# 48 in place of 32 blocks of the expert table u beside the selection, and 1.2 row fetches with each in place of 1.1

## The chip, the cores and the metric

The kernel runs on one core of one Trainium2 chip. Its time is in device microseconds from the start of the program to its end; three runs gave 3198.60, 3206.87 and 3208.08 us, so the median is 3206.87 us. The engines are named as the profile names them: PE is TensorE (PEld its weight loads), DVE is VectorE, ACT is ScalarE, POOL is GpSimd, and SP only issues transfers.

## The reference

One layer of a sequence model on 512 rows of width 2048, all in float32. A projection feeds a short convolution and a matrix memory, a second projection and a layer norm follow. The last part, in which the change lies, is a product-key lookup ("PEER"): for each row and each of 8 heads, 16 experts out of 16384 are picked by two top-16 searches over 128 keys; then

```
q  = h @ wq;  s = q . keys;  top 16 x top 16 -> top 16 experts eid, gate = softmax(top_s)
act = gelu(u[eid] . h)              # u: 16384 x 2048
ff  = sum over heads, experts of (gate * act) * v[eid]     # v: 16384 x 2048
out = LN(2^(1/4) * h + ff)
```

## The kernel before

The lookup is done in two ways at once. For 288 of the 512 rows ("columns" of the products) the kernel doesn't gather: it multiplies all of u with them, block by block (128 blocks of 128 experts), takes the gelu, multiplies it by a dense weight matrix that holds the gate of the picked experts and zero elsewhere, and multiplies the result with all of v. For the other 224 rows (128 of the first row tile, 64 and 32 of the second) it fetches the 128 picked rows of u and of v from HBM by indirect DMA, one fetch of 128 rows (1 MB) per slot, and DVE forms the dot product (line 558) or adds the weighted row (line 571). These fetches are a list of jobs, 462 with some others, and `advance(n)` issues n more of them after each block of the products, wherever the kernel is by then.

Every product is done in three passes, high times high, low times high, high times low. So each 1 MB block of a weight goes through `load_split`: a transfer on SP's queue (line 101), ACT rounds it to `hi` (line 109), DVE subtracts to get `lo` (line 110), and PE does 16 x 3 matmuls of 288 columns on it (lines 116 to 118).

The program has these stretches at the place of the change:

- The top-16 searches, on DVE, up to about 1230 us.
- The **selection stage** (1227 to about 1645 us). It multiplies the first `AHEAD` blocks of u (`u_chunk`), writes their gelu to DRAM (`hs_d`, line 904), and beside each block it takes some jobs from a second list: three `select` (DVE), three `spread`, and 72 *builds*. A build makes the weight matrix for 4 columns: DVE compares (line 848, `oa`) and scales (line 851, `ob`) one-hot matrices in bf16, PE multiplies them in 12 matmuls (line 858), ACT copies the result (line 861). After every 8 builds a 2 MB store goes to DRAM (line 896). The second list is taken by a power of the block's number: `len(jobs) * ((c + 1) / (AHEAD - 1)) ** 1.4`, so it is empty one block before the last.
- `MORE` = 4 more blocks of u, and then the **product stage** (to about 3120 us): 15 groups of 8 blocks of v (`v_part`), 4 more pieces of v, and the rest of u between them. Each of these is a *turn* that ends with `advance(rest / (turns - 4))`, `rest` being the slot jobs that are left.

`group_chunks` pairs the blocks that were done ahead with later ones: a group of v needs 8 blocks of gelu, and in the first `(AHEAD + MORE) / 4` groups 4 of them come back from DRAM (line 942) and 4 are multiplied in the group before; in later groups all 8 are. So a group of the first sort has 12 turns (8 of v, 4 of u), one of the second sort 16.

The order of instructions on an engine is not the order of the code: a scheduler lays out each engine's queue from priorities (the split of a block has a raised priority, `PRIO`) and estimated times, and the engines then run in that order. Fetches are tied to the last product in front of them for that layout alone.

The loop of the selection stage:

```
for c in range(AHEAD):
    gl = u_chunk(c, t2)
    nc.scalar.dma_start(hs_d[c], gl)
    upto = min(len(jobs), int(len(jobs) * min(1.0, (c + 1) / (AHEAD - 1)) ** POW + 1e-6))
    while done < upto:
        jobs[done]()
        done += 1
    advance(RATE_MID, 2 * NSLOT)
```

Of the kernel before, what the change touches and what calls it, by code (L numbers as in the profile page):

```python
# [37 lines left out]
TGRP = [(0, REST), (REST, P), (REST + P, P)]  # L38
TG = 32
NTG = ND // TG  # L40
AHEAD = 32
MORE = 4
NSLOT = 128
GL = 4
# [2 lines left out]
PRIO = 1000  # L47
LAG = 6
RATE_PROJ = 1.9
RATE_MID = 1.1  # L50
VW = P + 1
HK = NH * TOPK

# [1 line left out]
def group_chunks():  # L55
    cut = AHEAD + MORE
    gs = [list(range(4 * g, 4 * g + 4)) + list(range(cut + 4 * g, cut + 4 * g + 4)) for g in range(cut // 4)]
    gs += [list(range(c, c + 8)) for c in range(2 * cut, 120, 8)]
    return gs + [list(range(120, 124))]
# [6 lines left out]
def tile_kernel(ctx: ExitStack, tc: tile.TileContext, x, lin_g, lin_b, w_rows, w_proj, w_v, w_gate, b_gate,  # L66
# [17 lines left out]
    w_d = dram.tile([NTG, P, NKEY * TG], F32, name="w_d")  # L84
    hs_d = dram.tile([AHEAD + MORE, P, ND], F32, name="hs_d")
    nM_d = dram.tile([NH, S], F32, name="nM_d")
# [493 lines left out]
    def advance(n, most=10 ** 9):  # L580
        done_jobs[1] = min(done_jobs[1] + n, most, len(sjobs))
        while done_jobs[0] < int(done_jobs[1]):
            sjobs[done_jobs[0]]()
            done_jobs[0] += 1
# [190 lines left out]
    def u_chunk(c, pool, nb=2):  # L775
        w = load_split(ut[c])
        ps = ph.tile([P, S], F32, name="ph")
        for k in range(KD):
            mm3(ps[:, :ND], [a[:, k * P:(k + 1) * P] for a in w], [a[:, k, DS] for a in h1T], k == 0, k == KD - 1)
        gl = pool.tile([P, ND], F32, name="gl", bufs=nb)  # L780
        ACT.activation(gl, ps[:, :ND], AF.Gelu)  # L781
        return gl

    with ExitStack() as p2:
# [116 lines left out]
        done = 0  # L901
# [9 lines that stand above are left out]
    with ExitStack() as p3:  # L911
# [19 lines left out]
        def load_w(g):  # L931
            t_ = g2.tile([P, NTG, 4, TG], F32, name="wt")
            nc.sync.dma_start(t_.rearrange("p g i t -> p g (i t)"),
                              w_d[:, :, g * 4 * TG:(g + 1) * 4 * TG].rearrange("g p f -> p g f"))
            wt[g] = t_

        def make_g(c):
            if c // 4 not in wt:
                load_w(c // 4)
            if c < AHEAD + MORE:  # L940
                gl = g2.tile([P, ND], F32, name="gl", bufs=GL)
# [88 lines left out]

        for c in range(AHEAD, AHEAD + MORE):
            nc.scalar.dma_start(hs_d[c], u_chunk(c, g2, GL))
# [142 lines left out]
```

## Time and profile before

| what | value |
|---|---|
| median of three runs | 3206.87 us |
| profiled execution, its own time | 3204.96 us |
| its span, first to last instruction | 3203.2 us |
| PE busy | 2941.0 us, 92% |
| DVE busy | 2784.5 us, 87% |
| ACT busy | 1153.6 us, 36% |
| moved by DMA | 1013.19 MB, mean 316 GB/s |

Busy time of an engine is the time in which at least one of its instructions is in flight. A matmul of 288 columns is shown with some 300 ns, but the next begins long before it ends, so a row's mean duration is not what one costs; the distance between the ends of two blocks is. A window of the trace gives for each engine the busy time and the count of instructions, then the clock that PE was granted (1.00 is 2.4 GHz, 0.50 is 1.2 GHz), the busy share of the 16 DMA engines and what they moved.

### The profile page before, as it was taken

To read this page: it belongs to the slowest core of one execution; us is meant where nothing else is said; L and a number is where in the kernel's file an instruction comes from. 1 tells how busy PE (TensorE), PEld (TensorE's weight loads), DVE (VectorE), ACT (ScalarE), POOL (GpSimd) and SP (SyncE) were. 2 spreads that over 40 slices of the span, in tenths; PEclk is the share of its full clock that TensorE was granted. 3 is DMA by queue.
4 is the path that set the end of the run, shared out by engine and by line. 5 is a ranking of instruction groups with operands and counts; after the bars stand their busy time and mean duration, and the time that the engine had idled before them with its cause. 6 is when DMAs were issued, how large, how long until landed. Compare 5 with 4: busy or idle time off the path is not lost.

```text
span 3203.2 us, 46126 instructions
## 1 busy us (share of the span) xinstructions
PE 2941.0 (92%) x18951; PEld 2762.3 (86%) x18951; DVE 2784.5 (87%) x3543; ACT 1153.6 (36%) x1195; POOL 853.3 (27%) x465
## 2 busy tenths in 40 slices
PE   6989898999988999997899999989999999899997
PEld 5767688999976899997799999989899999899895
DVE  7997988889887799988778989988888989888888
ACT  5765523333332233332343333333323333333333
POOL 0000024433432001303023433423343333334322
PEclk9999999999999999998999999999999999999999
DMA  7996678889998335768599999989999999899994
GB/s 275 328 353 246 223 273 318 324 328 334 348 360 318 114 123 205 281 263 325 215 341 384 380 377 386 394 338 384 359 368 360 379 366 392 328 371 350 365 336 145
DMA packets 188085, 1013.19 MB, mean 316 GB/s; under 512 B 18194, under 2 KB 68386, under 8 KB 70178
## 3 DMA queue, kind: packets, MB, share of 16 engines
q1 hardware_dynamic: 112976, 500.29, 43.0%
q0 software_dynamic: 64512, 469.79, 37.1%
q10 hardware_dynamic: 10386, 40.17, 3.4%
q8 instruction: 148, 2.42, 0.3%
q14 instruction: 63, 0.52, 0.0%
HBM read 974.08 MB, written 34.68 MB: 315 GB/s over the span
## 4 chain that ended last, share of the span: by engine, by line
PE 40%; DMA 26%; DVE 25%; issue 7%; ACT 2%; POOL 0%; DVEq 0%; ACTq 0%; SPq 0%; POOLq 0%
DMA gt<-in_v_dram,idx 11%; DMA gt<-in_u_dram,idx 10%; DVE lo L110 10%; PE po L118 5%; PE po L117 5%; PE po L116 5%; PE acc L117 4%; PE acc L118 4%; PE acc L116 4%; PE ph L118 3%; PE ph L117 3%; PE ph L116 3%; DVE gt L558 3%; PE pw L858 2%; ACT hi L109 2%
## 5 line engine op out<-in xcount | busy, mean ns | idle before, releaser
L109 ACT ACTIVATE hi<-raw 128x2048 fp32r<-128x2048 f32 (+1 forms) x515 | 825.7, 1620 | 1208.8 <-PE po L117 379.5
L110 DVE TENSOR_TENSOR lo<-raw,hi 128x2048 fp32r<-128x2048 f32 (+1 forms) x515 | 981.9, 1921 | 98.0 <-ACT hi L109 96.2
L118 PE MATMUL ph<-tth,lo 128*128 128x288 f32 (+3 forms) x2336 | 706.3, 302 | 34.2 <-DVE lo L110 34.2
L116 PE MATMUL ph<-tth,hi 128*128 128x288 f32 (+3 forms) x2336 | 704.5, 302 | 14.5 <-ACT gl L781 10.1
L117 PE MATMUL ph<-ttl,hi 128*128 128x288 f32 (+3 forms) x2336 | 704.8, 302 | 0.4 <-DVE rsa L131 0.4
L549 POOL DMA_INDIRECT gt<-in_u_dram,idx x224 | 422.0, 1884 | 925.2 <-PE ph L118 236.3
L118 PE MATMUL po<-gh,lo 128*128 128x288 f32 x1984 | 597.9, 302 | 54.6 <-DVE lo L110 54.6
L549 POOL DMA_INDIRECT gt<-in_v_dram,idx x224 | 404.9, 1807 | 909.6 <-DVE rows L571 263.9
L558 DVE SCALAR_TENSOR_TENSOR gt<-gt,rows 128x2048 f32<-128x2048 f32 x224 | 510.1, 2285 | 127.1 <-DMA gt<-in_u_dram,idx 124.7
L571 DVE SCALAR_TENSOR_TENSOR rows<-gt,wts,rows 128x2048 f32<-128x2048 f32 x224 | 525.7, 2347 | 106.2 <-DMA gt<-in_v_dram,idx 105.6
L117 PE MATMUL po<-glo,hi 128*128 128x288 f32 x1984 | 596.1, 301 | 13.0 <-DVE glo L950 12.9
L116 PE MATMUL po<-gh,hi 128*128 128x288 f32 x1984 | 591.6, 301 | 2.7 <-ACT gh L949 2.6
L118 PEld LDWEIGHTS ph<-tth,lo 128*128 128x128 f32 x2336 | 443.9, 190 | 41.3 <-DVE lo L110 41.2
L116 PEld LDWEIGHTS ph<-tth,hi 128*128 128x128 f32 x2336 | 444.3, 190 | 15.9 <-ACT gl L781 10.9
L117 PEld LDWEIGHTS ph<-ttl,hi 128*128 128x128 f32 x2336 | 444.2, 190 | 0.5 <-DVE ttl L157 0.5
L118 PEld LDWEIGHTS po<-gh,lo 128*128 128x128 f32 x1984 | 381.9, 193 | 62.9 <-DVE lo L110 62.8
L117 PEld LDWEIGHTS po<-glo,hi 128*128 128x128 f32 x1984 | 381.7, 192 | 16.2 <-DVE glo L950 15.9
L116 PEld LDWEIGHTS po<-gh,hi 128*128 128x128 f32 x1984 | 380.3, 193 | 5.1 <-ACT gh L949 4.9
L116 PE MATMUL acc<-tth,hi 128*128 128x384 f32 x768 | 260.0, 339 | 0.0
L118 PE MATMUL acc<-tth,lo 128*128 128x384 f32 x768 | 258.5, 337 | 0.4 <-DVE lo L110 0.4
L117 PE MATMUL acc<-ttl,hi 128*128 128x384 f32 x768 | 258.5, 337 | 0.0
L949 ACT ACTIVATE gh<-gl 128x288 fp32r<-128x288 f32 x128 | 55.7, 441 | 379.0 <-DVE gl L945 370.1
(311 smaller groups left out, 3409.0 us busy)
## 6 DMA issues: line engine op xcount, KB each, us to landing
raw<-in_ut_dram SPq DMA_DIRECT2D x128, 1024.0 KB
raw<-in_vb_dram SPq DMA_DIRECT2D x128, 1024.0 KB
raw<-in_w_rows_dram SPq DMA_DIRECT2D x56, 1024.0 KB
raw<-in_w_proj_dram SPq DMA_DIRECT2D x48, 1024.0 KB
raw<-in_w_out_dram SPq DMA_DIRECT2D x32, 1024.0 KB
w_d<-wg ACTq DMA_DIRECT2D x9, 2048.0 KB
wt<-w_d SPq DMA_DIRECT2D x32, 576.0 KB
raw<-in_w_qrows_dram SPq DMA_DIRECT2D x16, 1024.0 KB
```

The lines of the kernel that those rows point to most:

```text
L109: ACT.activation(hi[:, c], raw[:, c], AF.Copy)
L110: DVE.tensor_sub(lo[:, c], raw[:, c], hi[:, c].bitcast(F32))
L116: last_mm[0] = PE.matmul(ps, a[0], b[0], start=start, stop=False)
L117: PE.matmul(ps, a[0], b[1], start=False, stop=False)
L118: PE.matmul(ps, a[1], b[0], start=False, stop=stop)
L549: ins = nc.gpsimd.indirect_dma_start(out=gt, out_offset=None, in_=src, in_offset=bass.IndirectOffsetOnAxis(ap=idx, axis=0))
L558: pend.append(lambda: DVE.scalar_tensor_tensor(gt, gt, 1.0, rows(), op0=OP.mult, op1=OP.mult, accum_out=dots[:, s:s + 1]))
L571: pend.append(lambda: DVE.scalar_tensor_tensor(rows(), gt, wts[:, s:s + 1], rows(), op0=OP.mult, op1=OP.add))
L858: m = PE.matmul(ps[:, s, :], bs[q][:, :, s], a[:, :, s], start=q == 2, stop=q == 0)
L949: ACT.activation(gh, gl, AF.Copy)
```

## The change

`AHEAD` goes from 32 to 48 and `RATE_MID` from 1.1 to 1.2. Sixteen blocks of u move from the product stage to the selection stage; the same 72 builds are spread over 48 blocks; the selection stage issues 57.6 slot jobs in place of 35.2. No arithmetic is added or taken away; 16 more blocks of gelu (144 KB each) are written to DRAM and read back. By `group_chunks`, 13 groups of v in place of 9 have 4 blocks done ahead; the order in which v lies in HBM follows.

```diff
-AHEAD = 32
+AHEAD = 48
 MORE = 4
...
 RATE_PROJ = 1.9
-RATE_MID = 1.1
+RATE_MID = 1.2
```

In the queues this shows at the end of the selection stage. SP's queue, the kernel before, around the last block of u that is loaded before the first block of v (`raw` is a block in transit, `wt` weights, `gl` gelu read back):

```order
L811 DMA kt<-in_keys_dram 128x128
L101 DMA raw<-in_ut_dram 128x2048 x37
L933 DMA wt<-w_d 128x9x128 x2
L101 DMA raw<-in_ut_dram 128x2048
L942 DMA gl<-hs_d 128x288 x2
```

And of the changed kernel:

```order
L811 DMA kt<-in_keys_dram 128x128
L101 DMA raw<-in_ut_dram 128x2048 x52
L933 DMA wt<-w_d 128x9x128 x2
L101 DMA raw<-in_ut_dram 128x2048 x2
L942 DMA gl<-hs_d 128x288 x2
```

In all, 40 blocks of u were loaded ahead of v and 56 are now. On PE's queue the builds sit between the matmuls of these blocks, and those that find no place run bare behind the 33rd block (the 48th now): 34 builds stand ahead of that point and 38 behind it in the kernel before, 43 and 29 in the changed one.

DVE's queue at that point, the kernel before, from the last split of a block (`lo`) on; `oa` and `ob` are the two steps of a build, `rows` is a fetched row added:

```order
L110 TENSOR_TENSOR lo<-raw,hi 128x2048
L851 TENSOR_TENSOR ob<-oa,tr 128x1536
L571 SCALAR_TENSOR_TENSOR rows_82<-gt,wts,rows_82 128x2048
L848 TENSOR_TENSOR oa<-iotab,tr 128x1024
L571 SCALAR_TENSOR_TENSOR rows_82<-gt,wts,rows_82 128x2048
L851 TENSOR_TENSOR ob<-oa,tr 128x1536
L571 SCALAR_TENSOR_TENSOR rows_82<-gt,wts,rows_82 128x2048
L848 TENSOR_TENSOR oa<-iotab,tr 128x1024
L571 SCALAR_TENSOR_TENSOR rows_82<-gt,wts,rows_82 128x2048
L851 TENSOR_TENSOR ob<-oa,tr 128x1536
L571 SCALAR_TENSOR_TENSOR rows_82<-gt,wts,rows_82 128x2048
```

Two more such rows of line 571 follow, then only builds. The changed kernel, from its last split on:

```order
L110 TENSOR_TENSOR lo<-raw,hi 128x2048
L848 TENSOR_TENSOR oa<-iotab,tr 128x1024
L571 SCALAR_TENSOR_TENSOR rows_82<-gt,wts,rows_82 128x2048
L851 TENSOR_TENSOR ob<-oa,tr 128x1536
L571 SCALAR_TENSOR_TENSOR rows_82<-gt,wts,rows_82 128x2048
L848 TENSOR_TENSOR oa<-iotab,tr 128x1024
L571 SCALAR_TENSOR_TENSOR rows_82<-gt,wts,rows_82 128x2048
L851 TENSOR_TENSOR ob<-oa,tr 128x1536
L571 SCALAR_TENSOR_TENSOR rows_82<-gt,wts,rows_82 128x2048
L848 TENSOR_TENSOR oa<-iotab,tr 128x1024
L851 TENSOR_TENSOR ob<-oa,tr 128x1536
```

Seven added rows stood behind the last split and four stand there now; ahead of it, from the start of the selection stage, 26 stood and 51 stand now (dot products of line 558 counted with them).

## Rows read from the trace of the kernel before

**Rows 1.** Busy time of each engine in windows, from the selection stage on.

```profile
core 0: us, PE busy (x) PEld busy (x) DVE busy (x) ACT busy (x) POOL busy (x), PEclk, DMA share, GB/s
1227.00:1498.00 271.00, 261.74 (x1982) 257.09 (x1980) 243.18 (x280) 100.64 (x112) 62.75 (x29) 0.99 0.75 281
1357.00:1392.00 35.00, 30.61 (x218) 29.79 (x218) 28.29 (x23) 10.55 (x13) 7.16 (x6) 0.90 1.00 399
1498.00:1517.00 19.00, 4.74 (x36) 3.88 (x36) 15.61 (x11) 1.79 (x3) 6.67 (x5) 0.62 0.81 304
1517.00:1575.00 58.00, 52.80 (x402) 42.77 (x403) 55.76 (x70) 19.79 (x33) 0.00 (x0) 0.95 0.38 161
1575.00:1645.00 70.00, 59.98 (x416) 58.08 (x414) 41.35 (x36) 23.92 (x28) 11.46 (x7) 0.93 0.88 308
1645.00:2337.00 692.00, 641.05 (x4628) 632.02 (x4627) 616.43 (x524) 229.78 (x213) 242.45 (x135) 0.97 0.97 376
2337.00:3016.00 679.00, 632.54 (x4610) 623.37 (x4609) 593.58 (x494) 220.40 (x197) 243.44 (x132) 0.98 0.95 365
```

**Rows 2.** Waits of DVE, 1645 to 3016 us (total us, times, longest).

```profile
DVE rows L571 <- DMA gt<-in_v_dram,idx: 77.8, 58, 4.1
DVE gt L558 <- DMA gt<-in_u_dram,idx: 53.5, 31, 4.0
```

**Rows 3.** Groups of instructions, 1645 to 3016 us (busy, mean ns, idle before).

```profile
L118 PE MATMUL po<-gh,lo 128*128 128x288 f32 x1799 | 543.2, 303 | 54.4 <-DVE lo L110 54.3
L118 PE MATMUL ph<-tth,lo 128*128 128x288 f32 x1280 | 381.6, 298 | 24.8 <-DVE lo L110 24.7
```

**Rows 4.** Groups of instructions, 1227 to 1498 us.

```profile
L116 PE MATMUL ph<-tth,hi 128*128 128x288 f32 x521 | 156.4, 300 | 4.4 <-ACT gl L781 4.4
L118 PE MATMUL ph<-tth,lo 128*128 128x288 f32 x522 | 156.0, 299 | 3.3 <-DVE lo L110 3.3
```

**Rows 5.** Timeline of DVE, 1483 to 1521 us: added rows behind the last split.

```profile
1486.48 2.28 DVE L110 TENSOR_TENSOR lo<-raw,hi 128x2048 fp32r<-128x2048 f32 x1
...
1500.73 2.35 DVE L571 SCALAR_TENSOR_TENSOR rows<-gt,wts,rows 128x2048 f32<-128x2048 f32 x1 [1.37 <-DMA gt<-in_v_dram,idx]
...
1515.00 2.35 DVE L571 SCALAR_TENSOR_TENSOR rows<-gt,wts,rows 128x2048 f32<-128x2048 f32 x1 [0.31 <-DMA gt<-in_v_dram,idx]
```

**Rows 6.** Chain of waits, 1519 to 1534 us: two builds in one round.

```profile
1525.74 1.59 PE pw L858 x12
...
1527.35 0.70 DVE oa L848
...
1528.08 0.97 DVE ob L851
...
1529.09 1.60 PE pw L858 x12
```

**Rows 7.** Timeline of ACT, 1600 to 1626 us: gelu of successive blocks of u.

```profile
1604.33 0.39 ACT L781 ACTIVATE gl<-ph 128x288 f32<-128x288 f32 x1
...
1610.73 0.39 ACT L781 ACTIVATE gl<-ph 128x288 f32<-128x288 f32 x1
...
1617.13 0.39 ACT L781 ACTIVATE gl<-ph 128x288 f32<-128x288 f32 x1
```

**Rows 8.** Chain of waits, 1300 to 1326 us: a build between matmuls of u.

```profile
1302.00 1.43 PE pw L858 x12
```

**Rows 9.** DMA, 1645 to 3016 us.

```profile
DMA packets 103728, 507.74 MB, mean 370 GB/s; under 512 B 8372, under 2 KB 44367, under 8 KB 44367
```

**Rows 10.** The whole trace's DMA view: a queue (packets, MB, share), then issues.

```profile
q0 software_dynamic: 64512, 469.79, 37.1%
...
raw<-in_ut_dram SPq DMA_DIRECT2D x128, 1024.0 KB
...
gl<-hs_d SPq DMA_DIRECT2D x36, 144.0 KB
```

**Rows 11.** Waits, 1227 to 1498 us.

```profile
DVE rows L571 <- DMA gt<-in_v_dram,idx: 13.2, 6, 4.8
```

**Rows 12.** Timeline of POOL, 1400 to 1530 us: the fetch after the longest pause.

```profile
1439.37 0.94 POOL L549 DMA_INDIRECT gt<-in_v_dram,idx  x1 [51.35 <-DVE rows L571]
```

## Prediction

> **What bounds the kernel now.** I read the windows first, because the change moves work from one stage to another and what matters is what each stage waits for. In the product stage (1645 to 3016 us) the DMA engines are busy 95 to 97% of the time at 365 to 376 GB/s, while PE is at 93% and DVE at 87 to 89% [rows 1]. There DVE waits 131 us for fetched rows (77.8 + 53.5) [rows 2], the next split stands behind the waiting instruction, and PE waits for the split: 54.4 + 24.8 us in the two largest groups [rows 3]. So this stage is set by transfers. The stretch of the selection stage from 1227 to 1498 us is another matter: PE is busy 261.74 of 271 us, and DMA only 75% [rows 1]. PE's waits in it are small [rows 4]; its one slow piece is 1357 to 1392 us, where DMA stands at 1.00 with 399 GB/s and PE loses some 4 us [rows 1]. Then come two poor stretches. From 1498 to 1517 us, the **hand-over**, PE is busy 4.74 of 19 us, because DVE adds rows at the pace at which fetches land [rows 1, 5]. From 1517 to 1575 us the **bare builds** run: 35 of them in 58 us (70 DVE instructions, two to a build) with DMA at 38% [rows 1], each waiting round DVE and PE [rows 6]. From 1575 to 1645 us the blocks that remain before v are multiplied.
>
> **The units.** A block of u costs PE 6.40 us when nothing disturbs it (1604.33 to 1610.73 to 1617.13) [rows 7]. A build among such matmuls costs PE 1.43 us [rows 8]. Two bare builds take 3.35 us (1525.74 to 1529.09), so one takes 1.68 [rows 6]. Bare added rows come every 3.57 us (1500.73 to 1515.00 is four steps) [rows 5]. A turn of the product stage costs (692 + 679) us over (4628 + 4610) / 48 = 192.5 turns, that is 7.12 us [rows 1], 0.72 over a block on PE alone.
>
> **The change, part by part.** The sum is made against the profiled execution's own 3204.96 us (span 3203.2, 1.8 us around it), which lies 1.9 us under the median of the runs.
>
> 1. *Fifteen more blocks and nine more builds ahead of the bare stretch* (33 and 34 in the order before, 48 and 43 now). On PE that is 15 x 6.40 + 9 x 1.43 = 108.9 us.
> 2. *What PE loses there.* Before, 33 x 6.40 + 34 x 1.43 = 259.8, so of 271 us 11.2 were lost, 0.34 a block. Added rows per block rise from 26 / 33 = 0.8 to 51 / 48 = 1.06; the product stage has 1.42 a turn and loses 0.72. On the line between these two the loss is 0.34 + 0.38 x (0.26 / 0.62) = 0.50, which gives 48 x 0.50 - 11.2 = +12.8 us. Bounds: at 0.34 a block +5.1, at the product stage's 0.72 it is +23.4. I take +12.8, by how far the rate of rows has gone from the one row to the other. DVE has room: its 243.18 us grow by 15 splits of 2.28, 25 rows of 2.35 and 9 builds of 1.67 (0.70 + 0.97), 108 us, to 351 of about 393, the same 90%. DMA has room too: 15 blocks, 25 fetches and 15 stores of 144 KB are 44 MB on top of 281 GB/s x 271 us = 76 MB, so 120 MB in 393 us, 306 GB/s.
> 3. *The hand-over.* Behind the last split stood seven added rows and stand four: 3 x 3.57 = -10.7 us. Bounds: nothing, if the fetches are late there too, and -19 if it goes altogether.
> 4. *The bare builds.* On PE's queue 38 builds stood behind the last block, and 29 do now: 9 fewer. One or two fewer fall in the hand-over, so 8 leave the bare stretch: -8 x 1.68 = -13.4 us (bounds -11.8 and -15.1, for 7 and 9).
> 5. *Before v.* Eight blocks in place of seven follow the bare builds: +6.4 us.
> 6. *The product stage* loses 16 turns. Four groups go from 16 turns to 12. Eight groups of 12 turns took 692 us, 86.5 each, six of 16 took 679 us, 113.2 each [rows 1], so 4 x 26.7 = -106.7 us. The slot jobs per turn stay: (462 - 125.4 - 35.2) / 212 = 1.42 before, (462 - 125.4 - 57.6) / 196 = 1.42 after (462 jobs in the list, 66 x 1.9 = 125.4 done before the stage). Bounds: by turns 16 x 7.12 = -114; by bytes, 16 blocks and 22.4 fetches of 1.049 MB each leave (a fetch is 469.79 MB / 448) and 16 reads of 0.147 MB come in, 37.9 MB, which at 370 GB/s is -102 us [rows 9, 10].
> 7. *Issues.* Sixteen more stores on ACT's queue and sixteen more reads on SP's: ACT is busy 100.64 of 271 us [rows 1] and SP only issues. Nothing, with that cover; if it were gone, 16 x 0.33 us.
>
> The sum is 108.9 + 12.8 - 10.7 - 13.4 + 6.4 - 106.7 = -2.7 us, so 3202.3 us. Nearly the whole of the move is paid back: a block costs PE in the selection stage about what a turn costs the DMA in the product stage, and the nine builds that leave the bare stretch still cost 1.43 us each among the blocks, against 1.68 bare. With every end of the bounds at once the sum lies between 108.9 + 5.1 - 19 - 15.1 + 6.4 - 114 = -27.7 and 108.9 + 23.4 - 0 - 11.8 + 6.4 - 102 = +24.9 us.
>
> One rule of the Trainium skill bears on part 6: the page "SBUF — State Buffer", section "A bandwidth-pool intuition that's wrong (but worth ruling out)", gives about 358 GB/s from HBM per core and calls HBM almost always the bottleneck end to end. The trace agrees for the product stage, a little above that figure (370 GB/s), and not for the selection stage (281 GB/s). By the page's figure the 37.9 MB would be worth an estimated 106 us.
>
> **The rivals.**
>
> *The selection stage stays on PE (faster).* The fetches land early enough that the loss stays at 0.34 a block (12.8 becomes 5.1), and for the same reason the four last rows find their data, so that the hand-over all but vanishes (-19 in place of -10.7). Then -2.7 - 7.7 - 8.3 = -18.7, 3186.3 us. For it: PE is at 97% over 271 us and DVE waits only 13.2 us for rows there [rows 1, 11]; 306 GB/s is far under 370. Against it: where the DMA queue filled, at 1357 us, PE lost time at once.
>
> *Rows wait on fetches (slower).* Twice as many rows are added in the stretch, each stands on DVE ahead of a split and of a build, and there are three fetch buffers. If the fetches keep the pace of the product stage's, the loss is 0.72 a block (+23.4 in place of +12.8) and the hand-over keeps its 19 us (+10.7): -2.7 + 10.6 + 10.7 = +18.6, 3223.6 us. It decides as soon as DVE waits for rows more than some 25 us in the stretch (twice the 13.2 of before, for twice the rows [rows 11]). For it: POOL issued no fetch for 51.35 us before 1439 us, since it waited for a buffer that DVE still held [rows 12], so the rows come in bursts. Against it: on average 1.06 a block is well under 1.42.
>
> *Only the bytes count (no difference).* If the product stage gives back bytes alone, 102 us, the sum is +2.0, 3207.0 us. For it: DMA at 97%. Against it: PE and DVE are idle in the same stretches, so a turn less frees them too.
>
> **How the numbers follow.** A measurement of this kernel tells a change from none at about 0.3%, 9.6 us. I give my forecast 0.43, the faster rival 0.27, the slower 0.20, the one by bytes 0.10. The forecast's own spread is about 9 us on each side, so of its 0.43 some 0.09 lie under -9.6 us and 0.03 above +9.6 us; of the faster rival 0.25 lie beyond the bound, of the slower 0.17; the rest is within it. So faster 0.34, same 0.46, slower 0.20. The likeliest time is 3202.3, given as 3202; the range of 8 in 10 reaches from under the faster rival's time, 3180, to just short of the slower one's, 3222.
>
> **What would show it.** In the changed kernel the stretch before the bare builds should be some 393 us long with PE at 94 to 96%; DVE's wait for fetched v rows in it about 20 to 25 us; the hand-over some 8 us; the bare builds 27 or so at 1.68 us, 45 us; the product stage, from the first v block's sum to the last group's, some 107 us shorter at the same 7.1 us a turn. A stretch of 383 us or less means the faster rival; one of 400 us with more than 30 us of waits for fetches means the slower. I am wrong in kind if a turn of the product stage changes by more than 0.1 us, since I hold it constant.

## The result, and the profile after

The changed kernel takes 3185.51 us (median of 8 runs, 3178.8 to 3198.7), the kernel before in the same runs 3207.47 us: ratio 0.993, 95% interval 0.9908 to 0.9952. That is 0.7% faster, 22 us, and clear of the noise. The forecast was 3202 and no difference, a sum of -2.7 us; the time is that of the faster rival (3186.3), and lies in the range.

The profiled execution of the changed kernel is the slowest of its eight (3198.70 us, span 3197.0). A second profile of each kernel was therefore taken (the first two experiments), and stages are compared over both. The stages are cut at the first gelu of a block of u and at the first and last sum of a v product. Windows of the kernel before, cut there (columns as in [rows 1]), first profile:

```profile
1234.00:1645.00 411.00, 372.90 (x2787) 355.70 (x2786) 348.99 (x362) 142.35 (x173) 79.19 (x40) 0.95 0.73 274
1645.00:3136.00 1491.00, 1389.50 (x10075) 1370.17 (x10074) 1317.28 (x1105) 487.39 (x441) 514.52 (x284) 0.98 0.96 368
```

The kernel before, second profile:

```profile
1240.00:1655.00 415.00, 373.28 (x2787) 355.85 (x2786) 348.72 (x362) 142.59 (x173) 82.56 (x40) 0.95 0.73 271
1655.00:3154.00 1499.00, 1394.45 (x10071) 1373.64 (x10070) 1317.92 (x1103) 486.68 (x440) 512.02 (x284) 0.97 0.96 366
```

The changed kernel, first profile:

```profile
1233.00:1739.00 506.00, 476.45 (x3550) 460.48 (x3550) 434.82 (x401) 178.07 (x205) 132.37 (x62) 0.97 0.81 305
1739.00:3130.00 1391.00, 1289.88 (x9311) 1271.75 (x9310) 1227.71 (x1065) 452.56 (x408) 497.53 (x262) 0.97 0.96 367
```

The changed kernel, second profile:

```profile
1237.00:1739.00 502.00, 473.69 (x3553) 457.03 (x3552) 434.29 (x405) 178.87 (x207) 138.98 (x62) 0.98 0.81 309
1739.00:3116.00 1377.00, 1282.63 (x9306) 1263.85 (x9305) 1225.63 (x1063) 451.78 (x406) 512.78 (x261) 0.98 0.97 371
```

The selection stage grew by 91 us (413 to 504, means of two), the product stage shrank by 111 (1495 to 1384). The selection stage moves 307 GB/s where it moved 273: the spare transfer time there is what was used. The turn of the product stage is unchanged, 1495 / 212 = 7.05 and 1384 / 196 = 7.06 us (by the turns among which the jobs are dealt; the 7.12 of the prediction counts the matmuls of a part of the stage). Of the 22 us these two account for 20.

Inside the selection stage, first profile of the changed kernel, against the first, third, fourth and fifth window of [rows 1]:

```profile
1227.00:1615.00 388.00, 372.55 (x2798) 366.83 (x2797) 347.30 (x330) 138.94 (x151) 118.89 (x54) 0.98 0.83 317
1615.00:1622.00 7.00, 3.55 (x29) 2.88 (x27) 5.88 (x5) 1.35 (x3) 1.87 (x2) 0.75 0.91 318
1622.00:1669.00 47.00, 42.55 (x324) 34.56 (x324) 43.62 (x55) 15.84 (x27) 0.00 (x0) 0.93 0.40 162
1669.00:1739.00 70.00, 63.15 (x443) 61.32 (x442) 43.92 (x38) 26.04 (x29) 13.30 (x7) 0.93 0.90 318
```

The stretch is 388 us (382 in the second profile) where 271 stood, PE still at 96%. The hand-over is 7 us where 19 stood. The 27 bare builds take 47 us where 35 took 58, the same 1.7 us each, two to a round as in [rows 6]. Waits of DVE for rows in that stretch, against [rows 11]:

```profile
DVE rows L571 <- DMA gt<-in_v_dram,idx: 25.2, 17, 3.4
```

It doubled, as the rows did (25.0 us in the second profile). And PE's idle time there, against [rows 4], in the groups of instructions:

```profile
L118 PE MATMUL ph<-tth,lo 128*128 128x288 f32 x758 | 228.4, 301 | 11.9 <-DVE lo L110 11.9
L116 PE MATMUL ph<-tth,hi 128*128 128x288 f32 x758 | 227.6, 300 | 2.2 <-ACT gl L781 2.2
```

PE waits 11.9 us for splits (8.9 in the second profile) where it waited 3.3, for half as many blocks again.

The rows that end the hand-over, in DVE's timeline, against [rows 5]: four come behind the last split (1603.99), the last at 1619.90, and they stand 3.75 us apart on average, 3.57 before.

```profile
1608.64 2.35 DVE L571 SCALAR_TENSOR_TENSOR rows<-gt,wts,rows 128x2048 f32<-128x2048 f32 x1 [1.75 <-DMA gt<-in_v_dram,idx]
1612.70 2.35 DVE L571 SCALAR_TENSOR_TENSOR rows<-gt,wts,rows 128x2048 f32<-128x2048 f32 x1 [0.83 <-DMA gt<-in_v_dram,idx]
1616.77 2.35 DVE L571 SCALAR_TENSOR_TENSOR rows<-gt,wts,rows 128x2048 f32<-128x2048 f32 x1 [1.11 <-DMA gt<-in_v_dram,idx]
...
1619.90 2.35 DVE L571 SCALAR_TENSOR_TENSOR rows<-gt,wts,rows 128x2048 f32<-128x2048 f32 x1
```

In the product stage DVE waits for rows 111.5 us where it waited 131.3 [rows 2], over 8% fewer turns (waits of DVE, 1739 to 3009 us):

```profile
DVE rows L571 <- DMA gt<-in_v_dram,idx: 56.7, 40, 4.7
DVE gt L558 <- DMA gt<-in_u_dram,idx: 54.8, 35, 4.1
```

And what its transfers move there, against [rows 9], is 38 MB less at the same rate:

```profile
DMA packets 100512, 470.05 MB, mean 370 GB/s; under 512 B 8014, under 2 KB 46030, under 8 KB 46030
```

### The profile page after: what moved, and what is told of

Read it like the earlier page. It is cut to its first block, busy times and chain, and to the rows that moved or that the text cites. A ratio compares the mean times of both kernels' runs of the same rounds, so it can differ in the third digit from the quotient of the medians.

```text
span 3197.0 us, 46184 instructions
## 1 busy us (share of the span) xinstructions
PE 2944.3 (92%) x18951; PEld 2767.0 (87%) x18951; DVE 2777.6 (87%) x3543; ACT 1154.9 (36%) x1195; POOL 893.5 (28%) x465
## 4 chain that ended last, share of the span: by engine, by line
PE 37%; DMA 27%; DVE 24%; issue 9%; ACT 2%; POOL 1%; ACTq 0%; DVEq 0%; SPq 0%; POOLq 0%
DMA gt<-in_u_dram,idx 12%; DMA gt<-in_v_dram,idx 11%; DVE lo L110 9%; PE po L118 4%; PE po L117 4%; PE po L116 4%; PE ph L118 4%; PE ph L117 4%; PE ph L116 4%; PE acc L117 3%; PE acc L118 3%; PE acc L116 3%; DVE gt L558 3%; PE pw L858 2%; DVE rows L571 2%
## 5 line engine op out<-in xcount | busy, mean ns | idle before, releaser
L549 POOL DMA_INDIRECT gt<-in_u_dram,idx x224 | 443.4, 1979 | 897.0 <-DVE gt L558 191.8
L549 POOL DMA_INDIRECT gt<-in_v_dram,idx x224 | 424.7, 1896 | 889.7 <-DVE rows L571 320.9
```

The lines of the kernel that those rows point to most:

```text
L549: ins = nc.gpsimd.indirect_dma_start(out=gt, out_offset=None, in_=src, in_offset=bass.IndirectOffsetOnAxis(ap=idx, axis=0))
```

## The experiments

Each changes a few constants of the kernel before, or the line that issues the fetches. Ratios are to the kernel before, run beside it. "Loss" is the stretch from the first matmul of u to the last one ahead of the bare builds, less 6.40 us for each block and 1.43 for each build in it. Stages, hand-overs and losses are read from one profiled execution of each, ratios from all runs; where that execution lies far from its median, it is said.

**Both kernels once more**, unchanged.

> The kernel before once more, unchanged, to see how far two profiles and two medians of one program lie apart. Both theories: ratio 1.000 within 0.3%. If run-to-run differences of some 10 us come from the product stage, its length (first to last sum of a v product, 1491 us in the first profile) moves by about that much while the selection stage (first gelu of u to first sum, 411 us) stays within 3 us.

Measured: 1.0003 (0.9982 to 1.0024). Selection stage 415 us against 411, product stage 1499 against 1491, and the start before them 6 us later. Two profiles of one program differ by some 8 us in the product stage, and by 4 in the selection stage, where 3 was the limit expected.

> The changed kernel once more, unchanged. Theory A (the parts of the prediction, the first profile being a slow draw of the product stage): selection stage again 507 us within 3 us, product stage shorter than the 1390 us of the first profile, by 10 to 18 us, time 3180 to 3192. Rival B (the selection stage itself varies with how the fetches land): selection stage differs by 5 us or more from 507 while the product stage stays.

Measured: 0.9931 (0.9903 to 0.9958), 3188.06 us. Product stage 1377 us, 13 shorter than in the first profile; selection stage 502 against 507. Theory A holds for the product stage and the time; its selection stage moved by B's 5 us, which are the smaller part. The loss in the stretch is 21 us in the first profile and 14 in the second, of one program.

**The two constants apart.**

```diff
-AHEAD = 32
+AHEAD = 48
```

> 48 blocks, rate left at 1.1: the blocks alone. Only 13 builds stand bare in this order, against 29 in the changed kernel. Theory A (sum of parts): 16 builds go from 1.68 to 1.43 us, -4 us; 4.8 fetches more are left to the product stage, 4.8 x 1.05 MB / 370 GB/s = +14 us; a little less loss beside the blocks, -3 us: about +7 us against the changed kernel, 3190 to 3195. Rival C (the bare builds are what costs, because no transfer of weight runs in them): -1.68 x 16 = -27 us and +14 us, so -13 us against the changed kernel, about 3172.

Measured: 1.0003 (0.9975 to 1.003), no gain at all. Both theories fail. The product stage was 1396 us, +12 against the changed kernel's mean, as expected for 4.8 more fetches. The selection stage was 513 us in place of some 497: bare builds and hand-over fell as laid out (13 builds), but the loss beside the blocks was 31 us, against 21 and 14 in the changed kernel. Some 11 us of that are lost in one place, 1540 to 1555 us:

```profile
1540.00:1555.00 15.00, 3.60 (x22) 3.01 (x20) 10.09 (x6) 3.00 (x4) 3.85 (x2) 0.67 0.86 356
```

PE is busy 3.6 of 15 us. What DVE does there, in its timeline: four added rows stood between two splits in the order, and the last three of them and the splits behind end the gap:

```profile
1541.44 2.35 DVE L571 SCALAR_TENSOR_TENSOR rows<-gt,wts,rows 128x2048 f32<-128x2048 f32 x1 [6.52 <-DMA gt<-in_v_dram,idx]
...
1548.13 2.35 DVE L571 SCALAR_TENSOR_TENSOR rows<-gt,wts,rows 128x2048 f32<-128x2048 f32 x1 [3.46 <-DMA gt<-in_v_dram,idx]
...
1551.00 2.35 DVE L571 SCALAR_TENSOR_TENSOR rows<-gt,wts,rows 128x2048 f32<-128x2048 f32 x1
1553.26 4.49 DVE L110 TENSOR_TENSOR lo<-raw,hi 128x2048 fp32r<-128x2048 f32 x2
```

It is a hand-over in the middle of the stretch: rows wait for fetches, and the split that PE needs stands behind them.

```diff
-RATE_MID = 1.1
+RATE_MID = 1.2
```

> 32 blocks, rate 1.2: the rate alone. 3.2 more fetches go to the selection stage; 37 builds stand bare against 38. Theory A: 3.2 x 2.83 us = -9 us in the product stage, +2 us beside the blocks: about 3200. Rival D (the rate is what gives the gain): 3190 or less. Rival E (only the number of blocks matters): 3207, no difference.

Measured: 1.0007 (0.9984 to 1.003), as rival E has it. It need not be because nothing moved: the product stage was 1489 us against 1495 and the selection stage 421 against 413, differences no larger than those between two profiles of one program, but the loss in it rose from 11 to 26 us. Most of the rise is one place here too. Ahead of the split at 1508.00 us DVE waits 8.9 us for a fetched row, and PE stands idle 10.3 us for that split (the first line is DVE's waits in the stretch, the second PE's: us in total, times, longest):

```profile
DVE rows L571 <- DMA gt<-in_v_dram,idx: 17.5, 6, 8.9
PE ph L118 <- DVE lo L110: 13.4, 4, 10.3
```

**The corners: all the blocks without the fetches, all the fetches without the blocks.** The change issues 57.6 slot jobs in the selection stage in place of 35.2.

```diff
-AHEAD = 32
+AHEAD = 48
-RATE_MID = 1.1
+RATE_MID = 0.7334
```

> 48 blocks with the 35.2 slot jobs of the kernel before (0.73 with each): the blocks alone move, no fetch does, so 301.4 jobs are left for 196 turns, 1.54 a turn. Theory K (above some 1.42 a turn the product stage goes by its fetches, about 2.7 us for each): 7.36 us a turn, product stage -52 us against before; selection stage like that of the run with rate 1.0, 487 us, +74: about +22 us, 3233. Rival L (a turn costs 7.05 us whatever the fetches): product stage -113, -39 us in all, 3172.

Measured: 1.0109 (1.0076 to 1.0142), 3239.38 us; selection stage 483 us, product stage 1446 us, 7.38 us a turn. Theory K on all three counts, within 6 us. (The profiled execution, 3228.61 us, is 11 us under the median, so the two stages together show 21 of the 35 us by which the runs are slower.) Windows of the two stages:

```profile
1229.00:1712.00 483.00, 468.27 (x3553) 458.55 (x3553) 387.18 (x381) 176.16 (x206) 73.63 (x40) 0.99 0.75 274
1712.00:3158.00 1446.00, 1315.77 (x9321) 1292.42 (x9320) 1273.15 (x1084) 451.39 (x406) 572.37 (x284) 0.95 0.96 369
```

DMA is at 369 GB/s in the product stage, where the kernel before has 368: with 1.54 fetches a turn it takes 0.33 us more for each turn, 2.8 us for each added fetch, which is 1.049 MB at 370 GB/s. The blocks alone save 49 us there, not the 111 of the whole change.

```diff
-RATE_MID = 1.1
+RATE_MID = 1.8
```

> 32 blocks with the 57.6 slot jobs of the changed kernel (1.8 with each): the fetches alone move, no block does; 279 jobs are left for 212 turns, 1.32 a turn. Theory K (under some 1.42 fetches a turn a turn of the product stage stays at about 7.02 us; beside 32 blocks DVE, 243 of 271 us busy, has no room for 22.4 rows of 2.35 us): product stage -7 us, selection stage +30 to +60 us, 3230 to 3260. Rival M (each fetch that leaves the product stage saves it 2.7 us, and costs little beside the blocks): -60 us in the product stage, +10 in the selection stage, 3160.

Measured: 1.0054 (1.0032 to 1.0075), 3226.14 us. Selection stage 453 us (+40), product stage 1475 (-20). M is out by far; it is near theory K, which had 3230 at least and -7 in the product stage. Eighteen added rows stand behind the last split there, and the hand-over became the longest seen, nearly all of it at 1.2 GHz. The two stages, and the hand-over:

```profile
1224.00:1677.00 453.00, 376.89 (x2791) 358.48 (x2790) 397.79 (x387) 143.22 (x174) 116.75 (x62) 0.89 0.81 299
1677.00:3152.00 1475.00, 1384.01 (x10077) 1367.41 (x10076) 1271.05 (x1083) 491.10 (x443) 454.27 (x262) 0.98 0.95 356
1512.00:1567.00 55.00, 13.28 (x102) 10.70 (x99) 47.43 (x33) 5.38 (x9) 20.01 (x15) 0.54 0.90 332
```

DVE is busy 47 of these 55 us: most of the hand-over is the rows' own time, 2.35 us each, and the smaller part is waits for fetches.

**More fetches at 48 blocks.**

```diff
+AHEAD = 48
+RATE_MID = 1.5
```

> 48 blocks, rate 1.5; 29 builds stand bare as in the changed kernel, so only the number of fetches differs: 14.4 more of them in the selection stage. Theory H (a fetch costs 2.83 us where transfers set the time, the product stage, and little beside the blocks, where PE sets it): product stage -41 us, selection stage +9 us, about -32 us against the changed kernel, 3155. Rival I (DVE is full beside the blocks, 347 of 382 us busy, so each further added row costs its 2.35 us and its waits there): selection stage +34 us or more, 3180 to 3190.

Measured: 1.0088 (1.0061 to 1.0116), slower than either theory. The product stage gave 8 us more, no more than two profiles differ by (1376 us, 7.02 a turn at 1.35 fetches), and 16 rows behind the last split made a hand-over of 50 us:

```profile
1631.00:1681.00 50.00, 11.83 (x92) 9.82 (x90) 40.08 (x28) 4.78 (x8) 18.00 (x13) 0.54 0.88 327
```

**Fewer bare builds, more bare builds.**

```diff
+AHEAD = 48
+RATE_MID = 1.0
```

> 48 blocks, rate 1.0; only 2 builds stand bare, against 29 in the changed kernel; 9.6 fetches fewer in the selection stage. Product stage +27 us in both theories. Theory A (a build costs 1.43 us beside the blocks and 1.68 bare): selection stage -12 us, 3203. Rival F (a build beside the blocks costs more than a bare one, 2.3 us by the run with 13 bare builds): selection stage +17 us, about 3230.

Measured: 0.9968 (0.9944 to 0.9991), 3203.42 us, where theory A had 3203 and F 3230. Two builds bare, loss 14 us, selection stage 487; product stage 1407 us at 1.47 fetches a turn, +24. (The profiled execution, 3192.19 us, is 11 us under the median.) Rival F is out: 27 builds more beside the blocks made the selection stage shorter by 17 us. Its windows of the stretch, and of what stands between that and the first v product (hardly a hand-over, and two bare builds):

```profile
1222.00:1643.00 421.00, 408.96 (x3137) 400.27 (x3137) 374.81 (x383) 154.75 (x179) 95.89 (x47) 1.00 0.77 289
1643.00:1716.00 73.00, 65.45 (x468) 63.89 (x466) 45.05 (x37) 26.44 (x30) 13.97 (x8) 0.93 0.94 326
```

PE is busy 97% of a stretch with 70 builds in it.

```diff
+AHEAD = 48
+RATE_MID = 1.2
-POW = 1.4
+POW = 5.0
```

> 48 blocks, rate 1.2, the builds taken later (power 5 in place of 1.4): 45 stand bare against 29, the fetches as in the changed kernel. Theory A: 16 builds go from 1.43 to 1.68 us, +4 us, 3192. Rival F: 16 builds go from 2.3 to 1.68 us, -10 us, 3178.

Measured: 0.9931 (0.9912 to 0.995), as the changed kernel. A's +4 us would be 0.994, F's -10 us 0.990, just under the interval: it speaks for A, weakly. The loss in the stretch was 32 us, but in an execution (3205.76 us) 20 us slower than the median of these runs.

```diff
+AHEAD = 56
+RATE_MID = 1.2
```

> 56 blocks, rate 1.2: 8 blocks more, and 1 build bare against 29. Product stage -56 us (8 turns of 7.05) in both theories. Theory A: selection stage +57 for the blocks, -7 for the builds, +4.5 lost beside them, -6 before v: -8 us against the changed kernel, 3180. Rival F: the 28 builds cost +17 us: about 3204.

Measured: 0.9942 (0.9923 to 0.996), 3193.92 us, between the two. The product stage was 1339 us, 45 less than in the changed kernel where 56 were expected; the loss beside the blocks was 32 us. Eight more blocks add nothing over 48.

**The hand-over alone.** The same number of fetches, but none beside the last blocks; in both, the line that issues them becomes

```diff
-            advance(RATE_MID, 2 * NSLOT)
+            advance(RATE_MID * AHEAD / 24 if c < 24 else 0, 2 * NSLOT)
```

with 24 of 32 blocks, and with 40 of 48 in the second.

> 32 blocks and 35.2 slot jobs as before, but all of these issued beside the first 24 blocks (1.47 with each), none beside the last 8; 3 added rows stand behind the last split in the order, against 7. Theory A (the hand-over is a loss of its own): hand-over 20 us to about 8, nothing else moves: -10 to -12 us, ratio 0.997 to 0.996. Rival J (rows that wait for their fetch cost PE the same wherever they stand): the stretch loses what the hand-over gains, ratio 1.000.

Measured: 0.996 (0.994 to 0.998): theory A by the time. The trace shows less: the hand-over fell from 20 to 1.5 us, but the loss in the stretch rose from 11 to 21, so the selection stage is 5 us shorter. By that, part of what the rows cost moved with them, as J has it; but the profiled execution (3212.45 us) is 15 us slower than the median, and whether the others lose as much in the stretch is not shown. Windows of the stretch and of the bare builds, which now follow it at once (against the first, third and fourth of [rows 1]):

```profile
1229.00:1510.00 281.00, 265.43 (x1981) 259.67 (x1980) 253.75 (x283) 100.13 (x112) 57.61 (x34) 0.97 0.77 286
1510.00:1575.00 65.00, 60.01 (x458) 48.58 (x456) 60.94 (x75) 22.17 (x38) 0.00 (x0) 0.97 0.42 173
```

> 48 blocks and 57.6 slot jobs as in the changed kernel, all issued beside the first 40 blocks (1.44 with each); no added row stands behind the last split (4 in the changed kernel), 21 builds bare against 29. Theory A: hand-over -7 us, 8 builds from 1.68 to 1.43, -2: about -9 us against the changed kernel, 3178. Rival J: no difference against the changed kernel, 3187.

Measured: 0.9958 (0.9935 to 0.9982), not faster than the changed kernel. Hand-over 0, bare builds 35 us, but the loss in the stretch 32 us:

```profile
1228.00:1640.00 412.00, 388.47 (x2909) 380.24 (x2908) 368.82 (x358) 143.36 (x159) 130.62 (x57) 0.97 0.83 313
1640.00:1675.00 35.00, 32.59 (x250) 26.43 (x247) 31.25 (x42) 12.53 (x22) 0.00 (x0) 1.00 0.35 141
```

Here A fails, and J is nearer. No version ran faster than the changed kernel.

By rate, the ratios at 48 blocks are 1.0109 (0.73), 0.9968 (1.0), 1.0003 (1.1), 0.993 (1.2) and 1.0088 (1.5). That is no smooth curve: nearly half of the gain is there at 1.0 already, and 1.1 lies above both its neighbours, with the gap at 1540 us in its trace.

## Why the prediction was right or wrong

*What bounds the stages* was right, and it is what decides. Four corners, selection and product stage in us:

| | 35.2 slot jobs there | 57.6 slot jobs there |
|---|---|---|
| 32 blocks | 413 + 1495, ratio 1 | 453 + 1475, ratio 1.0054 |
| 48 blocks | 483 + 1446, ratio 1.0109 | 504 + 1384, ratio 0.993 |

Neither the blocks alone nor the fetches alone gain, both lose; together they gain 22 us. The blocks need the fetches: a turn that leaves the product stage saves 7.05 us only if its 1.42 fetches leave with it, else the rest of the turns carry them at 2.8 us each. And the fetches need the blocks: beside 32 blocks, with DVE busy 94% of the stretch, 11 of the 22 added rows pile up behind the last split. That DVE has no room is argued, not shown: at 48 blocks and rate 1.5 as many pile up with DVE busy 87%, so the order alone can do it, and 57.6 slot jobs beside 32 blocks with none beside the last of them were not run. The prediction's step 6 said that the fetches per turn stay at 1.42, and took the turn as constant on that ground. It holds: 7.05 and 7.06 us, where two profiles of one program differ by 0.04 and 0.07.

*Step 6, the product stage*, -106.7 forecast, -111 measured (-100 and -122 for the pairs of profiles, so the two can't be told apart). Its premise, that groups with four blocks ahead are dearer per turn, holds in the changed kernel too: twelve such groups took 1043 us, 7.24 a turn, the two others 227, 7.09 (first profile):

```profile
1739.00:2782.00 1043.00, 966.54 (x6955) 952.81 (x6953) 917.95 (x788) 340.39 (x309) 377.78 (x200) 0.97 0.97 371
2782.00:3009.00 227.00, 208.13 (x1513) 205.13 (x1514) 202.09 (x188) 74.59 (x68) 89.30 (x45) 0.98 0.96 364
```

*Steps 1 and 2, blocks and builds*, +121.7 forecast (108.9 and 12.8), measured +115 (272 to 386, means of two, from the first to the last matmul). The 108.9 stands; the loss was too high: +12.8 forecast, +6 measured (+10 and +1 for the pairs). *This is the term that was furthest off*: step 2 drew a line from the loss per block to the number of rows per block. The runs show no such line. In the order of rows per block (two values where there are two profiles; the last column is the longest single wait of DVE for a row in the stretch):

| blocks, rate | added rows per block | loss per block, us | longest wait, us |
|---|---|---|---|
| 48, 0.73 (blocks alone) | 0.70 | 0.28 | none |
| 32, 1.1 (before) | 0.8 | 0.34, 0.38 | 4.8, 6.9 |
| 32, 1.2 | 0.91 | 0.80 | 8.9 |
| 48, 1.0 | 0.94 | 0.29 | 2.6 |
| 32, none after 24 blocks | 0.94 | 0.65 | 5.9 |
| 48, 1.1 | 1.02 | 0.65 | 6.5 |
| 48, 1.2 (changed) | 1.08 | 0.45, 0.29 | 3.4, 3.4 |
| 48, 1.2, power 5 | 1.10 | 0.67 | 10.4 |
| 56, 1.2 | 1.14 | 0.57 | 5.3 |
| 48, 1.5 | 1.15 | 0.89 | 8.0 |
| 32, 1.8 | 1.18 | 0.95 | 6.5 |
| 48, none after 40 blocks | 1.19 | 0.67 | 4.4 |

About one row a block goes with anything from 0.3 to 0.8 us of loss a block. Nor does the sum of DVE's waits for rows tell it: 25 us in the changed kernel, 23 with rate left at 1.1. The longest single wait goes with it better, from 48 blocks on at least: up to 3.4 us where little is lost, 4.4 and more where much is. That is a pattern over the traces, followed through to PE in two places, the gaps near 1500 us (32 blocks, rate 1.2) and 1540 us (48 blocks, rate 1.1). How much of it is the order of the rows and how much differs from one execution of a program to the next stays open: most of these are one profile each, the low values at 0.70 and 0.94 come from executions 11 us faster than their medians, and those of power 5 and of the stop after 24 from executions 20 and 15 us slower. In the stretch itself the forecast had 393 us, and under 383 for the faster rival; the two profiles have 388 and 382.

*Step 3, the hand-over*, -10.7 forecast, -13 measured (20.4 to 7.2 us). The rows behind the last split, which the order tells, give its length roughly: 3 rows 1 to 4 us, 4 rows 7, 7 rows 14 to 21, 16 rows 50, 18 rows 55; some 3.5 to 5 us for each beyond three. The prediction put this to the pace at which fetches land. That is the smaller part: DVE is busy 15.6 of the 19 us in the kernel before, 40 of 50 and 47 of 55 in the long ones. The rows' own 2.35 us each, ahead of the build steps that PE needs next, make most of it.

*Step 4, the bare builds*: -13.4 forecast, -13.4 measured (60.1 to 46.7). *Step 5*, +6.4 forecast, +3 measured. *Step 7*: nothing forecast, nothing seen.

All four misses went the same way, 17 us in sum, and that is the distance from the forecast of no difference to a gain of 20. The two large ones, in steps 2 and 6, are no larger than what two profiles of one program differ by; that the sum is real is shown by the medians, whose interval leaves 15 us of gain at least. The forecast is the difference of two sums of some 130 us, and an error of 5 to 8% on each was enough to hide the gain. The faster rival's time was right and its mechanism half: the loss per block did stay where it was and the hand-over shrank, though it didn't vanish; the rest of its gain is step 6. The slower rival's sign, more than 25 us of waits for rows in the stretch, was reached (25.2) without its consequence: DVE has the time, as long as the rows are spread.

The product stage runs at 366 to 371 GB/s at 1.42 and at 1.54 fetches a turn, so above 1.42 its transfers set the time. Below that they do so less: at 1.35 and 1.32 fetches a turn it moves 359 and 356 GB/s and takes 7.02 and 6.96 us a turn, under 1 us for each fetch that leaves; what bounds it then was not taken apart. The rule of the Trainium skill, page "SBUF — State Buffer", section "A bandwidth-pool intuition that's wrong (but worth ruling out)", gives about 358 GB/s from HBM per core and calls HBM almost always the bottleneck end to end. The trace agrees that transfers bound this stage, at a rate 2 to 4% above that figure; whether HBM or the DMA engines, busy 96%, set the rate no run here shows.

## What to carry to other kernels

When work of two kinds shares a stage, move both kinds in the proportion in which that stage is bound by them; one of them alone leaves the other to set the time. To size such a move, count what every remaining turn has to carry, and read from the order of the queues how many instructions that use fetched data stand together ahead of one that another engine needs: their number, and not their average rate, gave the length of the hand-over. A constant in a schedule that moves nothing by itself may still be half of a gain.

## What the runs showed of the hardware that was not expected

During a hand-over the granted clock of PE falls: 0.62 over 19 us in the kernel before, 0.54 over 50 and 55 us in the two long ones, with PE busy 4.7 us of the 19 and 12 to 13 us of the long ones; 0.54 is nearly all of it at 1.2 GHz. In the bare builds that follow, in which PE is busy over 90% of the time, it is back at 0.95, 0.93 and 0.96. Two profiles of one program differ by 8 and 13 us in the product stage at the same order of instructions, more than the effect that was forecast.
